# The last two parts of a convolution's x and C by seven products ahead of retention, with their weight sums made in DRAM

## The chip, the cores and the metric

One Trainium2 chip, one core. The time is device microseconds of one execution of the whole kernel; the kernel before has three timed runs. A profiled execution, timed apart from these, gives the trace. TensorE is called PE, VectorE DVE, ScalarE ACT, GpSimd POOL and SyncE SP.

## What is computed

One layer of a hybrid encoder for x of 512 tokens x 1024 channels, in float32. Cut to what matters here:

```python
h = rmsnorm(x, g_mix)
xc, gb, gc, q, k, v, g_sw, gate_a, gate_r = split(h @ w_in)       # 11 x 1024 columns
u = gc * xc
conv = sum over 3 taps of u_pad[:, tap:tap + s] * w_conv[tap]      # depthwise, along the tokens
y_a = (gb * conv) @ w_a_out
ret = retention of 4 heads (q, k rotated; scores with decay; @ v)  # both directions
y_r = (groupnorm(ret) * g_ret * silu(g_sw)) @ w_r_out
x = x + (sigmoid(gate_a) * y_a + sigmoid(gate_r) * y_r) @ w_o
x = x + swiglu(rmsnorm(x, g_ffn))                                  # 2816 wide
y = rmsnorm(x, g_final)
```

The change touches xc and gc (called x and C below), gb (called B) and the order in which they are worked out beside the retention.

## The kernel before

**Numbers.** Every matrix product is made of three matmuls: both operands are split into a rounded part hi and a remainder lo, and hi·hi, hi·lo and lo·hi are added up in PSUM (`mm3` and `prod`). A weight unit of 128 x 1024 goes from DRAM by SP's queue into a `raw` buffer (10 of them), ACT casts it to `whi` (L196) and DVE subtracts to get `wlo` (L197); five buffers of each exist. The same helper `split` makes hi and lo of activations.

**Products.** The plain ones take blocks of weights from `wpack`: `feature_major` gives 256 columns of a projection, with features on the partitions, as 2 x 24 matmuls of 128x512 (two units of weights); `token_major` gives an output product in four PSUM banks, 96 matmuls of 128x512 for 1024 columns in two halves. The others make a 2x2 block product by seven products instead of eight. `fm_quad` does it with features on the partitions: its seven calls of `prod` have 24 matmuls of 128x256 each, 168 in all, one unit of weights each, and it yields 256 columns of two projections at once, for both halves of the tokens. Their weights are `b11`, `b21`, `b22` and the sums `t1` to `t4` of quarters of w_in. For all quads but two, DVE adds the two raw quarters of a sum in SBUF (L300). For the first two pairs of the FFN (`SUMMED`) the sums are made in DRAM ahead of time by POOL's queue: `sum_step` issues one step from the list `steps` (a copy at L273, or an addition at L271), each put behind a store with `issue_after`. A step on a sum waits for the step before it on the same sum. The seven products write three PSUM banks (a, d, b); between products, ACT copies a bank into a `t512` buffer (`snap`, L432). There are nine `t512` buffers; the z stores read from them too.

**Stages.** The stages run in this order: projections q and k of three heads; six token-major quads for v, the head gates and the merge gates (`do_quad`, with the `sum_step` calls); `mix_quads`; the retention heads, with the last two parts of the convolution between them; output product of the convolution by `strassen`; merge; w_o; FFN; final norm.

The convolution is cut into four parts of 256 columns. In `mix_quads` three `fm_quad`s make x and C of part 0, x and C of part 1, and B of both parts; `conv` (L737 on ACT, L739 on DVE) applies the taps, and `z_forms` makes the sums of z = B * conv that the output product needs, splits them into t512 buffers and stores them to DRAM by POOL's queue (`store`, L601). Parts 2 and 3 are made by `do_mix(s)`: three `feature_major` calls with x, C and B, 48 matmuls of 128x512 each; x is snapped, C is multiplied with it (L774), the taps are applied, and B multiplies the result (L779).

The order of the heads is: `load_head(0)`, scores of head 0 (`do_scores`, 24 matmuls; DVE L833), `do_mix(2)`, and then for each head h: load of head h+1, `do_pv(h)` (48 matmuls; normalisation by DVE at L854 to L859), scores of head h+1, `do_t(h)` (16 transposes on DVE at L211, then splits with DVE at L200), and behind that `do_mix(3)` for h = 0, or else the output product wr(h-1) of the head before (`do_wr`, 96 matmuls).

**What sets the order.** Each engine works in the order of its own queue. The weights' order is the list `plan()`, taken one chunk at a time, split two units ahead and loaded four entries ahead. A scheduler places the instructions of all engines from the program's order and its priorities, so the order around a change is that of the built program.

Of the kernel before, what the change touches and what calls it, by code (L numbers as in the profile page):

```python
# [1 line left out]

# [1 line left out]

# [32 lines left out]
QH = CH // 2  # L37
# [33 lines left out]
def plan():  # L71
# [8 lines left out]
    def a(name, col):  # L80
        out.append(("c", name, 0, 8, col, 256))
# [16 lines left out]
            a("w_in", C_K + h * QK)  # L98
    for c in (0, 512):
        quad(C_GA + c, C_GR + c)  # L100
    for c0, c1 in ((C_XC, C_GC), (C_XC + 256, C_GC + 256), (C_GB, C_GB + 256)):
        for name in FORMS:
            out.append(("q", ("x", c0, c1), name, 0, 4))
    for s in (2, 3):
        for c in (C_XC, C_GC, C_GB):
            a("w_in", c + s * 256)
    for h in range(HEADS):
        for c in (0, 512):
            b("w_r_out", h * VD, 4, c, 512)
# [34 lines left out]

SUMMED = (("f", 0), ("f", 1))


def loads():  # L150
# [17 lines left out]
def block_kernel(ctx: ExitStack, tc: tile.TileContext, xT, xtok, wpack, wquad, cols, decs, rot, g_ffn, g_final, out):  # L168
# [45 lines left out]
    pos = [0]  # L214
    block = [0]

    made = []
    ready = []

# [8 lines left out]
    def prefetch_block(pieces, loads, splits, inbig):  # L228
        i = block[0]
        block[0] += 1  # L230
        st = [rawtile(), rawtile()]
        units = []
        per = max(1, pieces // 2)
        m = QH // per
        for c, (o, n) in enumerate(((0, 512), (512, 512), (QH, QH)) if pieces > 2 else ((0, QH), (QH, QH))):
            if loads:
                loads(c)
            nc.sync.dma_start(st[o // QH][:, o % QH:o % QH + n], wpack[i][:, o:o + n])
        for half in range(2):
# [16 lines left out]
    def quarter(quad, name, u=0):  # L256
        return wquad[next(i for i, x in enumerate(QUARTERS) if x[1:4] == (quad, name, u))]

    steps = [(quad, f, g, add) for group in (
        (("t1", "b11", 0), ("t3", "b22", 0)), (("t1", "b12", 1), ("t3", "b12", 1)),  # L260
        (("t2", "t1", 0),), (("t2", "b22", 1),), (("t4", "t2", 0),), (("t4", "b21", 1),))
        for quad in SUMMED for f, g, add in group]

    def sum_step(behind=None):

# [334 lines left out]
    def store(dst, t):  # L600
        return nc.gpsimd.dma_start(dst, t)  # L601
# [103 lines left out]
    def do_quad(left, right, func, func_left=None):  # L705
        def ev_sum(dst, o, f):
            def ev(tt, t):
                if f:
                    nc.scalar.activation(t, t, f)
                last = store(dst[:, o + tt, :], t)  # L710
                if tt and not o:
                    sum_step(last)
            return ev

        def ev21(tt, ps):
            t = t512()
# [32 lines left out]
    def z_forms(s, z):  # L749
# [3 lines left out]
        def put(j, t):  # L753
# [11 lines left out]
        put(2, w)  # L765
        put(3, x2[:, 1:2])

    def do_mix(s):
        us, c = [], bigtile()[:, 0:2, :]
        feature_major(xg, lambda m, ps: us.append(snap(ps)))  # L770
        u = u_tile()

        def ev_c(m, ps):
            nc.vector.tensor_tensor(out=u[:, m, 1:513], in0=ps, in1=us[m], op=ALU.mult)  # L774
            conv(m, 2 * s + m, u[:, m], c[:, m])
        feature_major(xg, ev_c)

        def ev_b(m, ps):
            nc.vector.tensor_tensor(out=c[:, m], in0=ps, in1=c[:, m], op=ALU.mult)  # L779
        feature_major(xg, ev_b)  # L780
        z_forms(s, c)

    T1, T2 = slice(0, 256), slice(256, 512)

    def halves(t):
        return t.rearrange("p (m t) -> p m t", m=2)

    def mix_quads():

        c = bigtile().rearrange("p (s m) t -> p s m t", s=2)  # L790
        for s in range(2):
            u, got = u_tile(), {}

            def ev21(ps):
                nc.vector.tensor_tensor(out=u[:, :, 257:513], in0=halves(ps), in1=halves(got["c2"]), op=ALU.mult)

            def ev12(t):
                nc.vector.tensor_tensor(out=u[:, :, 1:257], in0=halves(got["x1"]), in1=halves(t), op=ALU.mult)
            fm_quad(xf, lambda t: got.update(x1=t), ev21, lambda t: got.update(c2=t), ev12)
            for m in range(2):  # L800
                conv(m, 2 * s + m, u[:, m], c[:, s, m])

        def times(s, t):
            def ev(b):
# [3 lines left out]
        fm_quad(xf, times(0, T1), times(0, T2), times(1, T2), times(1, T1))  # L808
        for s in range(2):
            z_forms(s, c[:, s])  # L810


    def load(src, dt=F32):
        t = bigtile(dt)
        nc.sync.dma_start(t if dt == F32 else t.bitcast(F32), src)
        return t

    def load_head(h):
# [79 lines left out]
    mix_quads()  # L898
    nxt = load_head(0)
    p = do_scores(nxt[0], nxt[1])  # L900
    vv, sg = split_v(nxt[2]), nxt[3]
    do_mix(2)
# [403 lines left out]
```

## Time and profile before

| | us |
|---|---|
| timed runs, median of 3 | 1028.52 |
| timed runs, lowest and highest | 1028.49, 1029.9 |
| profiled execution, its own time | 1031.7 |
| its span | 1029.9 |
| mean clock of PE granted in it | 0.996 |

The span is what the trace covers; the profiled execution's own time is 1.8 us longer, for what lies around it. In the views that follow, a group's row has its busy time, the mean of one instruction in ns, and behind the second bar the idle time of its engine ahead of it and what ended most of that. A row of the timeline has start, length, engine, line and operation; in square brackets stands the idle time before it and what ended it. The chain of work that ended last is followed back from the last instruction. A row of the table by stages gives, for a stretch of time, the busy time and the number of instructions of PE, PE's weight loads, DVE, ACT and POOL, then the clock that PE was granted (1.00 is full), the share of the DMA engines' time and what they moved in GB/s. The heads stage begins at 386.6 us and the output product of the convolution at 605.2 us.

### The profile page before, as it was taken

The page shows a single profiled execution, that of the slowest core. Times are in us where ns is not written, and L with a number is a line of the kernel's source. Part 1 is how long each engine was busy: PE and PEld are TensorE (multiplying, and loading weights), DVE is VectorE, ACT ScalarE, POOL GpSimd, SP SyncE. Part 2 cuts the span into 40 slices and gives each one's busy share as a digit, 9 for nine tenths or more (in the row PEclk, how much of TensorE's full clock was granted, in tenths as well). Part 3 has the DMA queues.
Part 4 walks back from the last instruction along what each step waited for, and adds up shares of the span by engine and source line. Part 5 has one row for each costly group of instructions (what it writes and reads, how often), then busy time and mean ns, then how long its engine had stood idle before and what let it go on. Part 6 is the DMA issues. An engine that isn't in the chain of part 4 may idle for free.

```text
span 1029.9 us, 14786 instructions
## 1 busy us (share of the span) xinstructions
PE 1018.8 (99%) x5616; PEld 890.0 (86%) x5616; DVE 885.7 (86%) x1145; ACT 534.0 (52%) x723; POOL 125.2 (12%) x205
## 2 busy tenths in 40 slices
PE   8999999999999999999999999999999999999997
PEld 7888888888888998888888888889998999899985
DVE  7778898979798888797989998569998999889996
ACT  6546655653655455343543234356654565556553
POOL 0030221222122003202011000000002000110011
PEclk9999999999999999999999999999999999999999
DMA  9424587695767657818177525633318522663422
GB/s 342 181 74 176 199 275 224 207 305 175 239 192 246 245 194 272 333 60 333 47 281 276 211 91 180 232 108 113 127 45 220 178 83 82 198 152 102 164 33 91
DMA packets 51448, 187.66 MB, mean 182 GB/s; under 512 B 6896, under 2 KB 6896, under 8 KB 47408
## 3 DMA queue, kind: packets, MB, share of 16 engines
q1 hardware_dynamic: 36736, 133.45, 37.4%
q0 software_dynamic: 14496, 53.23, 17.4%
q8 instruction: 44, 0.72, 0.3%
q14 instruction: 28, 0.23, 0.1%
q10 hardware_dynamic: 144, 0.03, 0.0%
HBM read 148.14 MB, written 46.92 MB: 189 GB/s over the span
## 4 chain that ended last, share of the span: by engine, by line
PE 98%; DVE 1%; DMA 0%; issue 0%; POOLq 0%; POOL 0%; SPq 0%
PE bank L425 36%; PE bank L381 28%; PE bank L340 11%; PE bank L342 11%; PE bank L341 11%; DMA raw<-wpack 0%; PE bank L997 0%; PE bank L948 0%; DVE xform L197 0%; DVE big L1198 0%; DVE wlo L197 0%; DVE big L1173 0%; POOLq L1302 0%; POOL fin L1186 0%; PE bank L535 0%
## 5 line engine op out<-in xcount | busy, mean ns | idle before, releaser
L196 ACT CAST whi<-raw 128x1024 fp32r<-128x1024 f32 (+1 forms) x289 | 294.3, 1034 | 280.9 <-PE bank L425 63.7
L197 DVE TENSOR_TENSOR wlo<-raw,whi 128x1024 fp32r<-128x1024 f32 (+1 forms) x290 | 343.8, 1201 | 79.3 <-ACT whi L196 78.8
L381 PE MATMUL bank<-xform,whi 128*128 128x256 f32 x1424 | 257.5, 283 | 0.0
L381 PEld LDWEIGHTS bank<-xform,whi 128*128 128x128 f32 x1424 | 222.2, 192 | 0.9 <-ACT t L432 0.5
L381 PE MATMUL bank<-xform,wlo 128*128 128x256 f32 x712 | 201.1, 283 | 0.0
L425 PE MATMUL bank<-whi,big 128*128 128x512 f32 x596 | 187.5, 390 | 0.0
L300 DVE TENSOR_TENSOR raw<-raw 128x1024 f32<-128x1024 f32 (+1 forms) x128 | 151.9, 1204 | 3.8 <-DMA raw<-wquad 2.6
L381 PEld LDWEIGHTS bank<-xform,wlo 128*128 128x128 f32 x712 | 136.5, 192 | 0.0
L425 PEld LDWEIGHTS bank<-whi,big 128*128 128x128 f32 x596 | 111.9, 188 | 24.0 <-ACT t L432 0.4
L425 PE MATMUL bank<-whi,xform 128*128 128x512 f32 x384 | 121.1, 389 | 0.0
L425 PE MATMUL bank<-wlo,big 128*128 128x512 f32 x298 | 116.0, 389 | 0.0
L432 ACT COPY t<-bank 128x512 f32<-128x512 f32 x105 | 60.9, 585 | 56.0 <-PE bank L381 29.7
L340 PE MATMUL bank<-big,whi 128*128 128x512 f32 x224 | 87.4, 392 | 2.1 <-DVE whi L196 2.1
L342 PE MATMUL bank<-big,wlo 128*128 128x512 f32 x224 | 87.7, 393 | 0.0
L341 PE MATMUL bank<-big,whi 128*128 128x512 f32 x224 | 87.4, 392 | 0.0
L425 PEld LDWEIGHTS bank<-whi,xform 128*128 128x128 f32 x384 | 72.1, 188 | 14.9
L425 PE MATMUL bank<-wlo,xform 128*128 128x512 f32 x192 | 74.8, 390 | 0.4 <-DVE wlo L197 0.4
L340 PE MATMUL bank<-whi,big 128*128 128x512 f32 x176 | 69.0, 392 | 0.0
L341 PE MATMUL bank<-wlo,big 128*128 128x512 f32 x176 | 68.5, 389 | 0.0
L342 PE MATMUL bank<-whi,big 128*128 128x512 f32 x176 | 68.1, 390 | 0.0
L425 PEld LDWEIGHTS bank<-wlo,big 128*128 128x128 f32 x298 | 56.0, 188 | 11.4
L340 PEld LDWEIGHTS bank<-big,whi 128*128 128x128 f32 x224 | 42.3, 189 | 11.1 <-issue 2.3
(183 smaller groups left out, 1387.1 us busy)
## 6 DMA issues: line engine op xcount, KB each, us to landing
raw<-wquad SPq DMA_DIRECT2D x132, 512.0 KB, 4.7
raw<-wpack SPq DMA_DIRECT2D x51, 512.0 KB, 6.4
z<-t POOLq DMA_DIRECT2D x24, 256.0 KB, 5.6
zform<-z POOLq DMA_DIRECT2D x6, 1024.0 KB, 6.5
v<-t POOLq DMA_DIRECT2D x16, 256.0 KB, 5.1
sg<-t POOLq DMA_DIRECT2D x16, 256.0 KB, 4.7
qh<-t POOLq DMA_DIRECT2D x16, 256.0 KB, 2.8
ql<-t POOLq DMA_DIRECT2D x16, 256.0 KB, 3.5
```

Source lines behind the costliest of these rows:

```text
L196: first = (round or nc.scalar.copy)(hi, src)
L197: nc.vector.tensor_tensor(out=lo, in0=src, in1=hi.bitcast(F32), op=ALU.subtract)
L300: nc.vector.tensor_tensor(out=t, in0=t, in1=raws[quad, more, u][:, 0:n], op=ALU.add)
L340: nc.tensor.matmul(ps, lh, rh, start=first, stop=False)
L341: nc.tensor.matmul(ps, lh, rl, start=False, stop=False)
L342: nc.tensor.matmul(ps, ll, rh, start=False, stop=last)
L381: nc.tensor.matmul(o, l[:, c], r[:, k], start=start and s == 0 and k == 0 and i == 0, stop=stop and k == 3 and i == 2, skip_group_check=True)
L425: nc.tensor.matmul(pss[tt], l, r[:, c], start=start and k == 0 and i == 0, stop=stop and k == n - 1 and i == 2, skip_group_check=True)
L432: nc.scalar.copy(t, ps)
```

## The change

x and C of parts 2 and 3 become two more `fm_quad`s (`xc_quad(2)` and `xc_quad(3)`), run in `mix_quads` behind the three that were there and behind `z_forms` of parts 0 and 1; `load_head(0)` is called between the two, and the loads of later weight blocks are put behind its last load (`behind`). Their results stay in a second big tile (`cs[1]`). `do_mix(s)` keeps B alone, one `feature_major` of 48 matmuls, and `z_forms`. The sums of weights of both new quads are made in DRAM, ahead of those of the FFN, so that `steps` has 32 entries in place of 16. `sum_step` is called once more in each `do_quad` (four times rather than three) and after each of the four stores in `z_forms`; the FFN's sums are thereby made partly between the z stores. Each new quad loads seven units of weights (two quarters more are read in DRAM for the sums) where part 2 or 3 had four for x and C.

```diff
-    for c0, c1 in ((C_XC, C_GC), (C_XC + 256, C_GC + 256), (C_GB, C_GB + 256)):
+    for c0, c1 in ((C_XC, C_GC), (C_XC + 256, C_GC + 256), (C_GB, C_GB + 256),
+                   (C_XC + 512, C_GC + 512), (C_XC + 768, C_GC + 768)):
         for name in FORMS:
             out.append(("q", ("x", c0, c1), name, 0, 4))
     for s in (2, 3):
-        for c in (C_XC, C_GC, C_GB):
-            a("w_in", c + s * 256)
+        a("w_in", C_GB + s * 256)
...
-SUMMED = (("f", 0), ("f", 1))
+XC = tuple(("x", C_XC + o, C_GC + o) for o in (512, 768))
+
+SUMMED = (*XC, ("f", 0), ("f", 1))
...
-            nc.sync.dma_start(st[o // QH][:, o % QH:o % QH + n], wpack[i][:, o:o + n])
+            with tc.issue_after(behind[-1].ins) if behind else nullcontext():
+                nc.sync.dma_start(st[o // QH][:, o % QH:o % QH + n], wpack[i][:, o:o + n])
...
-    steps = [(quad, f, g, add) for group in (
-        (("t1", "b11", 0), ("t3", "b22", 0)), (("t1", "b12", 1), ("t3", "b12", 1)),
-        (("t2", "t1", 0),), (("t2", "b22", 1),), (("t4", "t2", 0),), (("t4", "b21", 1),))
-        for quad in SUMMED for f, g, add in group]
+    def sums_of(quads):
+        return [(quad, f, g, add) for group in (
+            (("t1", "b11", 0), ("t3", "b22", 0)), (("t1", "b12", 1), ("t3", "b12", 1)),
+            (("t2", "t1", 0),), (("t2", "b22", 1),), (("t4", "t2", 0),), (("t4", "b21", 1),))
+            for quad in quads for f, g, add in group]
+
+    steps = sums_of(SUMMED[:2]) + sums_of(SUMMED[2:])
...
-                if tt and not o:
+                if tt:
                     sum_step(last)
...
             for d, x in zip(zd[j], hl):
-                store(d[:, :, s, :], x.bitcast(F32))
+                last = store(d[:, :, s, :], x.bitcast(F32))
+            sum_step(last)
...
-    def do_mix(s):
-        us, c = [], bigtile()[:, 0:2, :]
-        feature_major(xg, lambda m, ps: us.append(snap(ps)))
-        u = u_tile()
-
-        def ev_c(m, ps):
-            nc.vector.tensor_tensor(out=u[:, m, 1:513], in0=ps, in1=us[m], op=ALU.mult)
-            conv(m, 2 * s + m, u[:, m], c[:, m])
-        feature_major(xg, ev_c)
-
-        def ev_b(m, ps):
-            nc.vector.tensor_tensor(out=c[:, m], in0=ps, in1=c[:, m], op=ALU.mult)
-        feature_major(xg, ev_b)
-        z_forms(s, c)
+    def xc_quad(s, c):
+
+        u, got = u_tile(), {}
+
+        def ev21(ps):
+            nc.vector.tensor_tensor(out=u[:, :, 257:513], in0=halves(ps), in1=halves(got["c2"]), op=ALU.mult)
+
+        def ev12(t):
+            nc.vector.tensor_tensor(out=u[:, :, 1:257], in0=halves(got["x1"]), in1=halves(t), op=ALU.mult)
+        fm_quad(xf, lambda t: got.update(x1=t), ev21, lambda t: got.update(c2=t), ev12)
+        for m in range(2):
+            conv(m, 2 * s + m, u[:, m], c[:, m])
...
         for s in range(2):
             z_forms(s, c[:, s])
-
+        xc_quad(2, cs[1][:, 0])
+        head = load_head(0)
+
+        behind.append(last[-1])
+        xc_quad(3, cs[1][:, 1])
+        return head
+
+    def do_mix(s):
+
+        c = cs[1][:, s - 2]
+
+        def ev_b(m, ps):
+            nc.vector.tensor_tensor(out=c[:, m], in0=ps, in1=c[:, m], op=ALU.mult)
+        feature_major(xg, ev_b)
+        z_forms(s, c)
```

Lines behind the diff's middle are eight to twenty higher in the changed kernel: L196 and L197 become L198 and L199, L340 to L342 become L348 to L350, L381 becomes L389, L601 becomes L609, L271 and L273 become L279 and L281, L211 becomes L213, L200 becomes L202, L779 becomes L826, L833 becomes L853.

Three places of the engines' orders matter for what follows. A row has line, operation, what it writes and what it reads, and the shape; names end in a buffer's number.

The first is DVE behind the scores of head 2, at the transposes of head 1 (`big_4384`). In the kernel before:

```order
L197 TENSOR_TENSOR big_4379<-big_4244,big_4378 128x1024
L197 TENSOR_TENSOR big_4333<-t512_4374,big_4332 128x512
L211 STREAM_TRANSPOSE big_4384<-big_3839 32x4x4x32 x16
L197 TENSOR_TENSOR wlo_4494<-raw_4486,whi_4493 128x1024
L200 SCALAR_TENSOR_TENSOR big_4402<-big_4384,cols_sb_89,big_4401 128x512 x4
L197 TENSOR_TENSOR wlo_4731<-raw_4726,whi_4730 128x1024
```

The same place in the changed kernel, where the transposes write `big_4595`:

```order
L199 TENSOR_TENSOR big_4544<-t512_4585,big_4543 128x512
L199 TENSOR_TENSOR big_4590<-big_4455,big_4589 128x1024
L213 STREAM_TRANSPOSE big_4595<-big_4190 32x4x4x32 x16
L199 TENSOR_TENSOR wlo_4637<-raw_4629,whi_4636 128x1024
L199 TENSOR_TENSOR wlo_4701<-raw_4696,whi_4700 128x1024
L202 SCALAR_TENSOR_TENSOR big_4613<-big_4595,cols_sb_97,big_4612 128x512 x4
L199 TENSOR_TENSOR wlo_4705<-raw_4697,whi_4704 128x1024
```

In both, one subtraction of a weight unit stands right behind the transposes. In the kernel before the units of wr0 were `wlo_4149`, `wlo_4153`, `wlo_4422` and `wlo_4426`, all of them ahead of this place, so that `wlo_4494` belongs to the next product. In the changed kernel wr0's units are `wlo_4360`, `wlo_4364`, `wlo_4633` and `wlo_4637`; the last of them has moved behind the transposes.

The second is PE in wr0, in the changed kernel, where the third unit of weights (`whi_4632`, `wlo_4633`) gives way to the fourth (`whi_4636`, `wlo_4637`):

```order
L348 MATMUL bank_4695<-whi_4632,big_4345 128x512
L349 MATMUL bank_4695<-wlo_4633,big_4345 128x512
L350 MATMUL bank_4695<-whi_4632,big_4346 128x512
L348 MATMUL bank_4692<-whi_4636,big_4345 128x512
L348 MATMUL bank_4693<-whi_4636,big_4345 128x512
L348 MATMUL bank_4694<-whi_4636,big_4345 128x512
L348 MATMUL bank_4695<-whi_4636,big_4345 128x512
L349 MATMUL bank_4692<-wlo_4637,big_4345 128x512
L350 MATMUL bank_4692<-whi_4636,big_4346 128x512
```

The four matmuls that need only `whi_4636` have moved ahead of the first one that needs `wlo_4637`; behind `wlo_4705` DVE's order is again that of the kernel before.

The third is POOL's queue at the z stores of parts 0 and 1, with nothing but stores in the kernel before:

```order
L601 DMA z020_222<-t512_3477 256x1x256
L601 DMA z120_223<-t512_3478 256x1x256
L601 DMA z021_224<-t512_3487 256x1x256
L601 DMA z022_226<-t512_3493 256x1x256
L601 DMA z121_225<-t512_3488 256x1x256
L601 DMA z013_228<-t512_3499 128x256
L601 DMA z122_227<-t512_3494 256x1x256
L601 DMA z113_229<-t512_3500 128x256
L601 DMA z020_222<-t512_3507 256x1x256
```

In the changed kernel the steps of the FFN's sums stand between them (`t2f0` is the sum t2 of FFN pair 0; L281 copies, L279 adds):

```order
L609 DMA z020_230<-t512_3502 256x1x256
L609 DMA z120_231<-t512_3503 256x1x256
L281 DMA t2f0_90<-t1f0_89 16x8192
L609 DMA z021_232<-t512_3513 256x1x256
L609 DMA z121_233<-t512_3514 256x1x256
L281 DMA t2f1_94<-t1f1_93 16x8192
L609 DMA z022_234<-t512_3520 256x1x256
L609 DMA z122_235<-t512_3521 256x1x256
L279 DMA t2f0_90<-wquad 64x2048
L609 DMA z013_236<-t512_3527 128x256
L609 DMA z113_237<-t512_3528 128x256
L279 DMA t2f1_94<-wquad 64x2048
```

After every two stores one step has moved in; the copy of `t2f0` stands ahead of the addition to it, and that ahead of the copy into `t4f0`.

More of the change, by code (lines that the diff above doesn't have):

```diff
@@ L1 @@
-from contextlib import ExitStack
+from contextlib import ExitStack, nullcontext
 import numpy as np
@@ L215, in block_kernel @@
     block = [0]
+    behind = []
     made = []
@@ L786, in halves @@
         return t.rearrange("p (m t) -> p m t", m=2)
+    def xc_quad(s, c):
[7 more added lines that the diff above has]
+            conv(m, 2 * s + m, u[:, m], c[:, m])
+    cs = []
     def mix_quads():
-        c = bigtile().rearrange("p (s m) t -> p s m t", s=2)
+        for _ in range(2):
+            cs.append(bigtile().rearrange("p (s m) t -> p s m t", s=2))
+        c = cs[0]
         for s in range(2):
[L792 to L801, printed above, removed]
+            xc_quad(s, c[:, s])
         def times(s, t):
@@ L810, in mix_quads @@
             z_forms(s, c[:, s])
+        xc_quad(2, cs[1][:, 0])
[9 more added lines that the diff above has]
+        z_forms(s, c)
+    last = []
     def load(src, dt=F32):
         t = bigtile(dt)
-        nc.sync.dma_start(t if dt == F32 else t.bitcast(F32), src)
+        last.append(nc.sync.dma_start(t if dt == F32 else t.bitcast(F32), src))
         return t
@@ L896, in do_wr @@
             token_major(yr, 0, 1, ev)
-    mix_quads()
-    nxt = load_head(0)
+    nxt = mix_quads()
     p = do_scores(nxt[0], nxt[1])
```

## The prediction

> **What bounds the kernel now.** I read the page's shares, then the chain of work that ended last, then the waits of TensorE.
>
> ```profile
> PE 1018.8 (99%) x5616; PEld 890.0 (86%) x5616; DVE 885.7 (86%) x1145; ACT 534.0 (52%) x723; POOL 125.2 (12%) x205
> PE 98%; DVE 1%; DMA 0%; issue 0%; POOLq 0%; POOL 0%; SPq 0%
> PE bank L340 <- DVE whi L196: 2.1, 1, 2.1
> PE bank L473 <- DVE lw L658: 1.0, 1, 1.0
> PE bank L425 <- DVE wlo L197: 0.4, 1, 0.4
> 326.49 55.14 PE bank L381 x456
> 605.23 38.08 PE bank L425 x168
> ```
>
> PE makes 98% of the chain and waits 3.5 us in all. So today each matmul less is time less, as long as PE is fed. The two chain rows are stretches of matmuls without a gap. They give the price of one: 38.08 / 168 = 226.7 ns for 512 columns, 55.14 / 456 = 120.9 ns for 256. The second thing to see is DVE at 86%: there is not much room behind PE. How much there is depends on the stage, and the table by stages shows it (span, PE, PEld, DVE, ACT, POOL busy, clock, DMA share, GB/s):
>
> ```profile
> 80.00:320.00 240.00, 239.60 (x1058) 198.07 (x1057) 208.68 (x225) 139.71 (x177) 50.10 (x88) 1.00 0.70 223
> 326.50:386.60 60.10, 60.10 (x491) 59.20 (x491) 54.15 (x65) 30.59 (x40) 4.09 (x7) 1.00 0.63 217
> 438.30:509.40 71.10, 71.10 (x315) 58.90 (x314) 62.98 (x97) 28.37 (x39) 7.57 (x13) 1.00 0.41 150
> ```
>
> These are the token-major quads with the sums in DRAM, the three quads of the convolution, and the stretch from the second head's scores to the end of the first output product's weights, with part 3 of the convolution in it.
>
> **Step 1, PE's own work.** Per part, 96 matmuls of 512 columns become 168 of 256: 96 x 0.2267 = 21.8 us against 168 x 0.1209 = 20.3 us. Two parts save 2 x 1.45 = 2.9 us. This is the whole gain.
>
> The Trainium skill ("TensorE: Matmul & The Clock Gate", section "Back-to-back issue gap") states a sustained spacing of about 131 ns at 512 columns and 81 ns at 128. An estimate by a straight line between its figures is 98 ns at 256, and by these the change would cost 2 x (168 x 98 - 96 x 131) ns = 7.8 us of PE rather than save any. The trace disagrees (226.7 and 120.9 ns), so the rows decide.
>
> **Step 2, the heads.** The gain of step 1 is not the main effect. PE loses 2 x 21.8 = 43.5 us of work between the heads, while most of what DVE did beside it stays. The groups of DVE in the stretch 438.3 to 509.4 (busy, mean ns, idle before and what ended it):
>
> ```profile
> L211 DVE STREAM_TRANSPOSE big<-big 32x512 f32<-32x512 f32 x32 | 22.5, 702 | 0.4
> L197 DVE TENSOR_TENSOR wlo<-raw,whi 128x1024 fp32r<-128x1024 f32 x7 | 8.6, 1222 | 3.2 <-ACT whi L196 3.1
> L833 DVE SCALAR_TENSOR_TENSOR t<-bank,tab 128x512 f32<-128x512 f32 x8 | 5.4, 685 | 0.4 <-PE bank L342 0.4
> L739 DVE SCALAR_TENSOR_TENSOR big<-u,cols_sb,big 128x512 f32<-128x512 f32 x4 | 3.0, 746 | 0.0
> L779 DVE TENSOR_TENSOR big<-bank,big 128x512 f32<-128x512 f32 x2 | 1.4, 692 | 1.1 <-PE bank L342 1.1
> L774 DVE TENSOR_TENSOR u<-bank,t 128x512 f32<-128x512 f32 x2 | 1.4, 684 | 0.0
> L197 DVE TENSOR_TENSOR t<-big,t 128x256 fp32r<-128x256 f32 x1 | 0.4, 427 | 2.4 <-DMA z<-t 2.4
> ```
>
> The two heads' transposes (22.5 us), the scores, the normalisation and the forms of z all stay. What leaves is two L774 (1.4), four L739 (3.0) and five of the seven subtractions of weight units, which the changed order has ahead of this stretch or behind it, 5 x 1.22 = 6.1 us: 10.5 in all. DVE is busy 62.98 us in 71.10, idle 8.1; of that idle time the waits named above make 0.4 + 3.2 + 0.4 + 1.1 + 2.4 = 7.5. So the work left is 71.1 - 7.5 - 10.5 = 53.1 us.
>
> PE's side: in the changed order, from the first scores matmul of head 1 to the first that reads the last weight unit of wr0, there stand 24 (scores) + 48 (B) + 48 (pv) + 24 (scores) + 72 + 4 (wr0) = 220 matmuls, 220 x 0.2267 = 49.9 us. That last unit's subtraction stands on DVE right behind the second transposes, as the rows of the order in the section on the change show; in the kernel before it was the unit of another chunk that stood there:
>
> ```profile
> 438.31 0.68 DVE L833 SCALAR_TENSOR_TENSOR t<-bank,tab 128x512 f32<-128x512 f32 x1
> 436.59 0.23 PE bank L340
> 496.77 11.44 DVE L211 STREAM_TRANSPOSE big<-big 32x512 f32<-32x512 f32 x16
> 508.25 1.23 DVE L197 TENSOR_TENSOR wlo<-raw,whi 128x1024 fp32r<-128x1024 f32 x1
> ```
>
> DVE takes up the scores 438.31 - 436.59 = 1.7 us after PE starts them. So the unit is ready 1.7 + 53.1 = 54.8 us after PE's start, where PE wants it at 49.9: PE waits **4.9 us**, if DVE itself never waits. The floor of this term is 4.9. Above it come the 2.4 us that DVE waits for a z store's buffer, which now falls in a shorter stage, and up to 1.8 us if DVE enters the stage late after conv, splits and B of part 2. The ends are 4.9 and 9.1; I take **7**, the middle. A part of it shows as a wait for wr0's PSUM banks, which the normalisation of pv1 frees. Behind these rows both orders agree, so the delay is carried to the end.
>
> **Step 3, the quads and the stores of z.** The fourth quad begins where the third ends, and its first snaps need t512 buffers that the z stores hold. Today's scores hide this (two waits of ACT, POOL's second store, and times from issue to landing):
>
> ```profile
> 395.37 0.62 ACT L196 CAST t<-t 128x512 fp32r<-128x512 f32 x1 [3.29 <-DMA z<-t]
> 398.82 0.62 ACT L196 CAST t<-t 128x512 fp32r<-128x512 f32 x1 [2.83 <-DMA z<-t]
> 385.09 0.68 POOL L601 DMA_DIRECT2D z<-t  x1 [0.43 <-DVE t L197]
> z<-t POOLq DMA_DIRECT2D x24, 256.0 KB, 5.6
> t2f<-t1f POOLq DMA_DIRECT2D x2, 512.0 KB, 6.1
> t2f<-wquad POOLq DMA_DIRECT2D x2, 512.0 KB, 8.9
> t4f<-t2f POOLq DMA_DIRECT2D x2, 512.0 KB, 5.2
> ```
>
> ACT already waits 3.29 and 2.83 us for z stores. Now eight steps of the FFN sums stand between these stores on POOL. Each copy or addition waits for the one before it in its chain: 6.1, then 8.9, then 5.2 us. From the second store's end, 385.1 + 0.7 = 386, the third step of a chain is issued at 386 + 6.1 + 8.9 = 401, and whatever stands behind it waits with it. PE reaches the fourth quad's third product, which overwrites the bank that its first snap reads, at 326.5 + 3 x 20.3 + 11.2 (93 x 0.1209: three products of its own and 21 matmuls of the fifth quad, which the order puts ahead) = 398.6. The snap stands on ACT behind casts at 398.82 or later, and the next snap needs the buffer of a store that follows such a cast and lands 5.6 us later, at 404. So PE waits somewhere between nothing (if the stores drain as today and the weights' buffers are free) and 8 us (if a store behind the 401 step is the one needed: 401 + 5.6 - 398.6). I take **4**, between the two; no row decides it more closely.
>
> **Costed at nothing.** Casts and subtractions of weight units rise from 8 to 14. Per quad DVE has now (54.15 - 12 x 1.204 for L300) / 3 = 13.2 us of 20.3, since the new quads have no L300 adds:
>
> ```profile
> L300 DVE TENSOR_TENSOR raw<-raw 128x1024 f32<-128x1024 f32 (+1 forms) x128 | 151.9, 1204 | 3.8 <-DMA raw<-wquad 2.6
> ```
>
> Eight more DRAM steps fall into 80 to 320. Each reads and writes 0.5 MB, 8.4 MB in all, 38 us at the 223 GB/s of that row, against 240 x 0.30 = 72 us of idle DMA. If that cover were gone, a late sum would stall the fourth quad at its second unit. The eight steps' issue time on POOL hides in its 190 idle us there. Head 0's loads now go out between the fourth and the fifth quad, about a quad's 20.3 us ahead of the scores, against landings of 7.4 to 11.1 us:
>
> ```profile
> big<-qh SPq DMA_DIRECT2D x4, 1024.0 KB, 7.4
> big<-sg SPq DMA_DIRECT2D x4, 1024.0 KB, 11.1
> ```
>
> **The sum.** -2.9 + 7 + 4 = +8.1 us on the profiled execution: 1031.7 + 8.1 = 1039.8. That execution was 3.2 us above the median of the runs (1028.52), so by the median I forecast **1036.6**; its ends are -2.9 + 4.9 + 0 and -2.9 + 9.1 + 8, so 1030.5 to 1042.7.
>
> **The rivals.**
> - Only the heads stall (step 3's cover holds; today PE runs through the first z stores without a wait): -2.9 + 7, **1032.6**. Against it stand ACT's two waits.
> - PE's clock falls at the new waits. The waits quoted at the start include one of 2.1 us, and behind it the clock reads:
>
> ```profile
> 7.00:11.40 4.40, 4.40 (x13) 3.44 (x14) 4.21 (x8) 4.03 (x7) 0.00 (x0) 0.62 1.03 383
> 84.29 0.50 PE L425 MATMUL bank<-wlo,xform 128*128 128x512 f32 x1 [0.40 <-DVE wlo L197]
> 84.30:88.00 3.70, 3.70 (x16) 3.09 (x17) 3.70 (x4) 2.49 (x4) 0.00 (x0) 1.00 0.00 0
> ```
>
>   A clock of 0.62 over 4.4 us loses 1.7 us; the 0.40 us wait lost none. Two or three waits of over 2 us would add 3.4 to 5.1: **1040.0 to 1041.7**. Against it: the slow clock at 7 us may come from the start of the program. The Trainium skill (the same page, "What's actually happening") says that an idle window of about 3.4 us halves the clock, and as much busy time restores it; by that only a wait in one piece of that length counts, and no row here shows one.
> - A balance: DVE gets 2 us of the stretch's work done during pv0, and step 3 costs nothing: stall 2.9, no change, **1028.5**.
> - The other side: PE stays covered in both places and the 2.9 us are gained, **1025.6**. This needs DVE's work in the stretch to be at most 49.9 - 1.7 = 48.2 us rather than 53.1, that is, over four more subtractions ahead of the second transposes. DVE was idle 8.1 us in the stretch, so it is not full today; but the idle time is already taken off above.
>
> That the change does not do what it says is excluded: the order shows both quads ahead of the scores.
>
> **Chances.** Forecast 0.52, heads only 0.17, clock 0.12, balance 0.08, faster 0.11. A measurement of this kernel can tell about 0.2% (2 us) from no change. Faster 0.11, same 0.08, slower 0.81. The range reaches from the balance to the upper end of step 3's bound with a little of the clock, 1028.0 to 1043.5; it leaves out the faster rival and a few hundredths above.
>
> **What would show it.** Step 1: 168 matmuls per new quad at 0.121 us without gaps. Step 2: waits of PE at wr0's first or last weight unit, behind DVE's transposes, of 5 to 9 us; wrong if PE runs through from the second scores to wr0's end. Step 3: a wait of PE in the fourth quad for ACT's snap, with ACT waiting for z stores; wrong if PE runs through or if the wait is for weights from DRAM. The clock: PEclk below 1.00 behind these waits. Were the sums in DRAM late, PE would wait in the fourth or fifth quad for a load of t1 to t4, and the whole reckoning would be too low.

## The result, and the profile after

| | median us | lowest and highest | runs |
|---|---|---|---|
| before | 1029.9 | 1028.49, 1030.16 | 5 |
| changed | 1055.52 | 1053.29, 1056.79 | 5 |

The ratio is 1.0248, with a 95% interval of 1.0234 to 1.0262: the changed kernel is 25 us slower. The prediction had the sign and said 1036.6 in a range up to 1043.5. The profiled execution took 1056.34 us, 24.6 more than that of before.

The page's shares and chain of the changed kernel, as they were shown of before:

```profile
PE 1024.6 (97%) x5760; PEld 900.5 (85%) x5760; DVE 894.3 (85%) x1157; ACT 541.2 (51%) x731; POOL 134.3 (13%) x221
PE 81%; DVE 10%; DMA 4%; issue 3%; ACT 1%; POOL 1%; POOLq 0%; SPq 0%; DVEq 0%; ACTq 0%
```

PE's share of the chain fell from 98% to 81%. PE is busy for longer although it has less to do, which already hints at a slower clock. Its waits (in all, times, longest):

```profile
PE bank L389 <- ACT t L440: 10.4, 2, 10.1
PE bank L349 <- DVE wlo L199: 4.7, 1, 4.7
PE bank L389 <- DVE wlo L199: 2.3, 2, 1.7
PE bank L389 <- ACT whi L198: 1.3, 2, 1.1
PE bank L348 <- DVE bnmv L875: 1.2, 1, 1.2
PE bank L348 <- DVE whi L198: 1.1, 1, 1.1
PE bank L481 <- DVE lw L666: 1.0, 1, 1.0
PE bank L348 <- DVE big L879: 0.8, 2, 0.4
```

L389 is the product of the quads: 10.4 + 2.3 + 1.3 = 14.0 us are lost there, 13.2 of them in the fourth and fifth quad and 0.8 in the ones ahead. The 4.7, 1.2 and 0.8 are lost at wr0, 6.7 us. The two that are left, 2.1 us, are the program's start; the kernel before waited 3.5 us in all, so 1.4 more. The table by stages shows where the clock goes down:

```profile
387.00:430.00 43.00, 29.80 (x205) 28.56 (x205) 20.31 (x29) 13.79 (x20) 14.30 (x21) 0.80 1.02 365
480.00:560.00 80.00, 73.38 (x311) 59.26 (x310) 74.23 (x121) 34.77 (x52) 10.28 (x18) 0.96 0.60 227
```

At the prices of the prediction (0.1209 and 0.2267 us) the 205 matmuls of 256 columns of the first would take 24.8 us and take 29.8; the 311 of 512 columns of the second would take 70.5 and take 73.4. So 5.0 + 2.9 = 7.9 us go to the clock. The account closes: -2.9 (fewer matmuls) + 14.0 + 6.7 + 7.9 - 1.4 = 24.3 us, against 24.6 measured. The first row also has DMA at its full share and 365 GB/s.

The long wait in the fourth quad, from the timeline of the changed kernel:

```profile
400.39 0.62 ACT L198 CAST t<-t 128x512 fp32r<-128x512 f32 x1 [3.28 <-DMA z<-t]
...
405.16 0.69 DVE L199 TENSOR_TENSOR t<-t,t 128x512 fp32r<-128x512 f32 x1 [5.48 <-DMA z<-t]
...
407.13 0.62 ACT L198 CAST t<-t 128x512 fp32r<-128x512 f32 x1 [6.12 <-DMA z<-t]
...
412.02 0.69 DVE L199 TENSOR_TENSOR t<-t,t 128x512 fp32r<-128x512 f32 x1 [6.17 <-DMA z<-t]
...
412.75 0.58 ACT L440 COPY t<-bank 128x512 f32<-128x512 f32 x1 [4.69 <-DVE t L199]
...
413.38 0.80 PE L389 MATMUL bank<-xform,whi 128*128 128x256 f32 x2 [10.12 <-ACT t L440]
413.98 0.41 PE L389 MATMUL bank<-xform,wlo 128*128 128x256 f32 x1
```

and the step of its chain ahead of these, with POOL's first wait for a step of the sums:

```profile
394.81 17.08 DMA z<-t
...
402.90 0.83 POOL L279 DMA_DIRECT2D t2f<-wquad  x1 [6.42 <-DMA t2f<-t1f]
```

Read it from the end: PE waits for ACT's snap (L440), the snap for a t512 buffer that DVE reads at 412.02, and that subtraction for a buffer whose z store was issued at 394.81 and landed 17.08 us later. Ahead of that ACT and DVE had waited for z stores before, ACT 3.28 and 6.12 us and DVE 5.48. The store that ended the wait was on its way before POOL waited for any step of the sums: in this stretch that first happened ahead of the step at 402.90, for 6.42 us. So it was issued without such a wait, and what was late is its landing. Behind the wait PE's matmuls are slow: the two of the row at 413.38 take 0.6 us rather than 0.24.

The heads, on DVE and PE:

```profile
518.25 11.45 DVE L213 STREAM_TRANSPOSE big<-big 32x512 f32<-32x512 f32 x16
529.73 2.36 DVE L199 TENSOR_TENSOR wlo<-raw,whi 128x1024 fp32r<-128x1024 f32 x2
...
531.00 0.79 PE L349 MATMUL bank<-wlo,big 128*128 128x512 f32 x1 [4.66 <-DVE wlo L199]
...
532.02 0.63 PE L349 MATMUL bank<-wlo,big 128*128 128x512 f32 x1
```

This is the place that the prediction named: wr0's last weight unit, behind the second transposes. The matmuls behind the wait are 0.43 us apart, not 0.227.

### The profile page after: what moved, and what is told of

It reads as the page before. It is cut to its first block, busy times and chain, and to the rows that moved or that the text cites. A ratio compares the mean times of both kernels' runs of the same rounds, so it can differ in the third digit from the quotient of the medians.

```text
span 1054.6 us, 15127 instructions
## 1 busy us (share of the span) xinstructions
PE 1024.6 (97%) x5760; PEld 900.5 (85%) x5760; DVE 894.3 (85%) x1157; ACT 541.2 (51%) x731; POOL 134.3 (13%) x221
## 4 chain that ended last, share of the span: by engine, by line
PE 81%; DVE 10%; DMA 4%; issue 3%; ACT 1%; POOL 1%; POOLq 0%; SPq 0%; DVEq 0%; ACTq 0%
PE bank L433 33%; PE bank L389 25%; PE bank L349 7%; PE bank L350 7%; PE bank L348 7%; DMA z<-t 2%; DVE big L213 2%; DVE wlo L199 2%; DVE big L199 1%; DMA ga<-t 1%; DVE big L747 1%; ACT whi L198 1%; DVE raw L308 1%; DVE t L853 1%; POOL z L609 0%
## 5 line engine op out<-in xcount | busy, mean ns | idle before, releaser
L198 ACT CAST whi<-raw 128x1024 fp32r<-128x1024 f32 (+1 forms) x295 | 300.5, 1034 | 290.6 <-PE bank L433 62.4
L199 DVE TENSOR_TENSOR wlo<-raw,whi 128x1024 fp32r<-128x1024 f32 (+1 forms) x296 | 350.7, 1202 | 81.2 <-ACT whi L198 80.7
L389 PE MATMUL bank<-xform,whi 128*128 128x256 f32 x1552 | 283.4, 285 | 10.7 <-ACT t L440 10.4
L389 PEld LDWEIGHTS bank<-xform,whi 128*128 128x128 f32 x1552 | 244.0, 194 | 12.4 <-ACT t L440 11.5
L389 PE MATMUL bank<-xform,wlo 128*128 128x256 f32 x776 | 220.5, 285 | 0.0
L389 PEld LDWEIGHTS bank<-xform,wlo 128*128 128x128 f32 x776 | 150.1, 194 | 0.0
L440 ACT COPY t<-bank 128x512 f32<-128x512 f32 x107 | 61.9, 585 | 58.0 <-PE bank L389 31.0
L433 PE MATMUL bank<-wlo,xform 128*128 128x512 f32 x192 | 74.8, 390 | 0.0
L348 PE MATMUL bank<-whi,big 128*128 128x512 f32 x176 | 69.1, 395 | 2.0 <-DVE bnmv L875 1.2
L350 PE MATMUL bank<-whi,big 128*128 128x512 f32 x176 | 69.2, 396 | 0.0
L433 PEld LDWEIGHTS bank<-wlo,big 128*128 128x128 f32 x298 | 56.0, 188 | 11.4
L348 PE MATMUL bank<-big,whi 128*128 128x512 f32 x160 | 63.0, 396 | 1.1 <-DVE whi L198 1.1
L350 PE MATMUL bank<-big,wlo 128*128 128x512 f32 x160 | 62.7, 394 | 0.0
L349 PE MATMUL bank<-big,whi 128*128 128x512 f32 x160 | 62.6, 394 | 0.0
L198 ACT CAST big<-t 128x512 fp32r<-128x512 f32 (+1 forms) x60 | 34.4, 579 | 26.1 <-DVE t L1072 12.1
```

The lines of the kernel that those rows point to most:

```text
L198: first = (round or nc.scalar.copy)(hi, src)
L199: nc.vector.tensor_tensor(out=lo, in0=src, in1=hi.bitcast(F32), op=ALU.subtract)
L348: nc.tensor.matmul(ps, lh, rh, start=first, stop=False)
L349: nc.tensor.matmul(ps, lh, rl, start=False, stop=False)
L350: nc.tensor.matmul(ps, ll, rh, start=False, stop=last)
L389: nc.tensor.matmul(o, l[:, c], r[:, k], start=start and s == 0 and k == 0 and i == 0, stop=stop and k == 3 and i == 2, skip_group_check=True)
```

## The experiments

All ratios are to runs of the kernel before on the same chip. Theories for the quads' term were Q (POOL's queue: the steps of the sums hold the z stores) and D (too much DMA in these 40 us); F (the order of the z forms and the snap) came when Q fell. For the heads they were H (DVE has more work than PE) and its rivals.

**1. e1_sums_later: the sums out of the z stores of parts 0 and 1.**

```diff
-            sum_step(last)
+            if s >= 2:
+                sum_step(last)
```

> The changed kernel with the eight FFN sum steps that stood between the z stores of parts 0 and 1 put between those of parts 2 and 3. In the changed kernel PE waits 13 us in the fourth quad and loses about 5 us more to a lower clock behind it. Theory Q (POOL's queue: each step waits for the step before it on the same sum, and the z stores behind it wait along): the wait falls to 0 to 3 us, the clock stays at 1.00 there, and the time goes from 1055.5 to about 1038 (1035 to 1041). Theory D (too much DMA at once, the loads of head 0 above all; the sums are a part of it only): the wait falls to 5 to 8 us, time 1044 to 1051.

Measured: 1057.26 us, ratio 1.0259 [1.024, 1.0278]. Nothing was won. Its longest waits of PE:

```profile
PE bank L389 <- ACT t L440: 6.1, 1, 6.1
PE bank L349 <- DVE wlo L199: 5.6, 1, 5.6
PE bank L389 <- DVE wlo L199: 4.7, 2, 4.2
```

and the stage of the quads in the table:

```profile
387.00:430.00 43.00, 31.03 (x220) 29.83 (x219) 21.48 (x31) 16.40 (x23) 9.04 (x14) 0.84 0.74 280
```

With no sum between the stores the quads still lose 12.4 us (6.1, 4.7 and 1.6 for casts). Theory Q falls as the cause by itself; the 5 to 8 us and the time that theory D gave did not come either. The steps seem to cost in their new place: PE waits 8.5 us at wr0 rather than 6.7, and 1.8 us for loads of a later head, for which the changed kernel doesn't wait.

**2. e2_head_early: head 0's loads ahead of the z forms.**

```diff
+        head = load_head(0)
         for s in range(2):
             z_forms(s, c[:, s])
         xc_quad(2, cs[1][:, 0])
-        head = load_head(0)
```

> The changed kernel with load_head(0) ahead of z_forms of parts 0 and 1, so that 4 MB are loaded before these stores. Theory Q: POOL's queue is as before, the wait in the fourth quad stays at 10 to 14 us, time 1053 to 1057. Theory D: the DMA share there falls from 1.02 to about 0.75, the z stores land in 7 us or less, the wait falls by 6 to 10 us, time 1043 to 1049.

Measured: 1047.84 us, ratio 1.0168 [1.0147, 1.019], 8 us better. In the quads PE waits 9.3 us:

```profile
PE bank L389 <- ACT t L440: 6.0, 2, 5.7
PE bank L389 <- ACT whi L198: 1.7, 2, 1.1
PE bank L389 <- DVE wlo L199: 1.6, 2, 1.0
```

The loads are a part of it, as theory D has it, and the time is in its range. But the share of DMA did not fall to 0.75 (0.97 in 387 to 430), the wait fell by 4.7 us and not by 6 to 10, and more than half of it is left. At wr0 4.6 us are left; the waits of 1.2 and 0.8 us for its banks went too, which is a part of the 8 us.

**3. e4_one_part: as 1, and only part 2 by a quad.** The plan, `SUMMED` and `mix_quads` have part 2 alone, and for part 3:

```diff
+        if s == 3:
+            us = []
+            feature_major(xg, lambda m, ps: us.append(snap(ps)))
...
+            feature_major(xg, ev_c)
```

> As e1_sums_later, but only part 2's x and C by a quad; part 3's stay between the heads as 2 x 48 matmuls of 128x512. Theory H (in the heads DVE has more work than PE): the 6.7 us of waits at wr0 and the 2.9 us of lower clock behind them vanish, against 1.45 us more PE work: 7 to 9 us under e1_sums_later, about 1030. Rival (the waits at wr0 come from elsewhere, the weights' loads or the sums between the stores of parts 2 and 3): the waits stay, 1 to 2 us above e1_sums_later.

Measured: 1041.21 us, ratio 1.0109 [1.0093, 1.0126], 16 us under 1. In the heads only 0.8 us of waits are left, the largest of them 0.6; in the quads it still waits:

```profile
PE bank L390 <- ACT t L441: 9.6, 3, 7.4
...
PE bank L349 <- ACT big L921: 0.6, 1, 0.6
```

The heads' term hangs on part 3's matmuls between them, as forecast. The gain is larger than the 7 to 9 us expected, since one quad less also shortens the quads' waits.

**4. e5_unit_first: as 1, wr0's last weight unit ahead of the transposes.**

```diff
+        if h == 1:
+            prefetch()
         new = do_t(h, t)
```

> As e1_sums_later, with one call of prefetch() ahead of the second transposes, so that the subtraction of wr0's last weight unit stands ahead of them on DVE. Theory H (DVE is short of time in all of the stage): the wait at wr0 goes but comes back at the next scores or output product, time within 2.5 us of e1_sums_later. Rival O (only the place of this one subtraction counts): 4.7 us of wait and about 2.9 us of clock are saved, 6 to 8 us under e1_sums_later.

Measured: 1056.33 us, ratio 1.0254 [1.023, 1.0277], the same as 1. The wait has only moved:

```profile
PE bank L348 <- ACT big L912: 5.0, 1, 5.0
```

L912 is ACT's copy of wr0's banks. It stands on ACT behind the splits of the transposed head, and these wait for DVE's transposes. The matmul that waits, at 537.44 us, reads no weights: wr0's 96 matmuls run through behind their first wait, and it is `do_pv(2)` behind wr0 that waits for wr0's banks to be copied out. So the wait came back in the product that follows, at the next thing behind the transposes. The time is as theory H said, the place one product earlier.

**5. e6_z_between: z forms of part 1 behind the fourth quad.**

```diff
-        for s in range(2):
-            z_forms(s, c[:, s])
+        z_forms(0, c[:, 0])
         xc_quad(2, cs[1][:, 0])
+        z_forms(1, c[:, 1])
```

> The changed kernel with z_forms of part 0 ahead of the fourth quad and z_forms of part 1 behind it (before: both ahead of it); sums and loads untouched. Theory F (the fourth quad's first snap stands on ACT behind the casts of both z_forms, and these need two turns of the nine t512 buffers, each as long as a z store takes to land): the waits in the fourth and fifth quad fall from 13 us to 4 or less, the clock stays near 1.00, time 1038 to 1044. Theory D (too much DMA in these 40 us): the same stores, sums and loads run, the waits stay at 9 us or more, time over 1048.

Measured: 1046.56 us, ratio 1.0167 [1.0149, 1.0184]. The fourth quad now runs through; of the two new quads only the fifth still waits, once, for the same kind of snap:

```profile
411.50 0.62 ACT L198 CAST t<-t 128x512 fp32r<-128x512 f32 x1 [7.52 <-DMA z<-t]
...
419.71 0.80 PE L389 MATMUL bank<-xform,whi 128*128 128x256 f32 x2 [6.22 <-ACT t L440]
```

Theory F is right that the order decides who waits, theory D that a z store still takes long: ACT waits 7.52 us for one. Neither range held; each has about half.

**6 to 8. The three together, and in pairs.** e7_quads_clear has the order of 5, the loads of 2 and the sums behind the loads of the merge gates:

```diff
-            sum_step(last)
...
-        nc.gpsimd.dma_start(t, d)
+        sga_load = nc.gpsimd.dma_start(t, d)
+    while steps:
+        sum_step(sga_load)
     do_wr(HEADS - 1, yr)
```

> As e6_z_between, with load_head(0) ahead of z_forms of part 0 and the eight FFN sum steps behind the loads of the merge gates, after the last head. If order, loads and sums are all of the quads' term: no wait over 1 us in the quads, clock 1.00 there, the waits of 5 to 7 us at wr0 and the clock behind them stay: 1034 to 1039. If something else holds the fourth quad: waits of 4 us or more there, 1042 or over.

e11_order_and_loads leaves the sums between the z stores:

> As e7_quads_clear, but with the FFN sum steps between the z stores, as in the changed kernel (so: z forms of part 0 and 1 apart, head 0 loaded early). With the order right and no surge of DMA, the sums should cost little if they only fill POOL's queue: wait in the quads 0 to 2 us, 1034 to 1038. If the sums hold the z stores by themselves: 3 to 7 us of waits there, 1038 to 1044.

e12_order_and_sums leaves the loads late:

> As e7_quads_clear, but with load_head(0) behind z forms of part 1, as late as in e6_z_between (so: order right, sums out of the way, 4 MB of head 0 loaded between the quads). If the loads alone hold the z stores and the scores: 3 to 7 us of waits in the quads or at the first scores, 1038 to 1044. If they cost little once sums and order are right: 1034 to 1038.

| kernel | z forms apart | head 0 early | sums later | ratio | PE's waits in the quads, us | clock, 387 to 430 | landing of a z store, us |
|---|---|---|---|---|---|---|---|
| changed | | | | 1.0248 | 14.0 | 0.80 | 7.4 |
| e1 | | | yes | 1.0259 | 12.4 | 0.84 | 9.0 |
| e2 | | yes | | 1.0168 | 9.3 | 0.88 | 5.4 |
| e6 | yes | | | 1.0167 | 6.7 | 0.88 | 7.4 |
| e12 | yes | | yes | 1.0088 | 1.9 | 1.00 | 6.5 |
| e11 | yes | yes | | 1.0049 | 2.1 | 1.00 | 5.1 |
| e7 | yes | yes | yes | 1.0045 | 1.4 | 1.00 | 3.5 |

The medians are 1034.38 us for e7 (interval of the ratio 1.0031 to 1.0059), 1034.91 for e11 (1.0031 to 1.0067) and 1038.32 for e12 (1.0073 to 1.0103). The landing is the median of the kernel's 24 stores of 256 KB. In e7 all of the 1.4 us are in the three old quads, and the two new ones run through; in e11 and e12 1.0 and 0.9 us are left in the new ones. e7's time came as expected, with 4.1 us at wr0 rather than 5 to 7, and e11 by its first case. e12 lies on the border of its two cases; its waits in the quads are short, and a part of its 4 us over e7 is at wr0, 6.3 us of waits against 4.1.

The table tells three things. Without the order no row is under 9 us of waits; but loads early and sums later were not run together in the old order, so it is not shown that the order is needed. With it, either the early loads or the later sums are enough for the quads. And the sums alone, which the prediction took for the cause, are worth nothing without the order (e1), 8 us with it and late loads (e6 to e12), and nothing again once the loads are early (e11 to e7).

The early loads shorten the landing of a z store in every pair of rows, and so do the later sums in the new order. The landing alone does not decide: with 5.4 us (e2) the quads wait, with 6.5 (e12) they hardly do. Nor does the share of DMA decide how long a store takes: in 387 to 430 us it is 0.74 in e1, with 9.0 us, and 1.01 in e11, with 5.1. So theory D's "too much DMA" is right about the loads, but what it is in them that lengthens a landing is not shown. The rows behind the first and the last figure, first of the changed kernel, with two steps of the sums:

```profile
z<-t POOLq DMA_DIRECT2D x24, 256.0 KB, 7.4
t2f<-t1f POOLq DMA_DIRECT2D x2, 512.0 KB, 8.3
t2f<-wquad POOLq DMA_DIRECT2D x2, 512.0 KB, 14.7
```

and of e7_quads_clear:

```profile
z<-t POOLq DMA_DIRECT2D x24, 256.0 KB, 3.5
```

**9. e8_pool_subtracts: as 6, eight subtractions of weight units on POOL.**

```diff
-            nc.vector.tensor_tensor(out=lo, in0=src, in1=hi.bitcast(F32), op=ALU.subtract)
+            (sub or nc.vector).tensor_tensor(out=lo, in0=src, in1=hi.bitcast(F32), op=ALU.subtract)
...
+made.append(split(..., sub=nc.gpsimd if wr and half else None))
```

> As e7_quads_clear, with the subtraction of every second weight unit of the four output products wr (8 units) on POOL rather than DVE. Theory H (DVE has more work than PE between the heads): 8 x 1.2 us less for DVE, the waits at wr0 fall from about 7 us to 2 or less and the clock stays up, time 1027 to 1031. Rival P (POOL is too slow at this, over 6 us a unit, or slows DVE): new waits for these units, not under e7_quads_clear.

Measured: 1035.71 us, ratio 1.0059 [1.0042, 1.0076], not under e7. Its subtractions on POOL, from the groups, and then its longest wait of PE:

```profile
L199 POOL TENSOR_TENSOR wlo<-raw,whi 128x1024 fp32r<-128x1024 f32 x8 | 19.9, 2491 | 77.8 <-ACT whi L198 77.8
```

```profile
PE bank L348 <- ACT big L910: 3.9, 1, 3.9
```

POOL takes 2.49 us for what DVE does in 1.2, and PE does not wait for it. But from the timeline, right ahead of the transposes:

```profile
496.36 2.65 POOL L199 TENSOR_TENSOR wlo<-raw,whi 128x1024 fp32r<-128x1024 f32 x1 [5.02 <-ACT whi L198]
496.64 3.46 DVE L199 TENSOR_TENSOR big<-big 128x1024 fp32r<-128x1024 f32 x1
```

A subtraction of DVE took 3.46 us rather than 1.2 while POOL made one of its own, so the transposes started at 500.0, against 498.4 in e7. DVE was not relieved ahead of them, and the wait moved to ACT's copies behind them, as in 4. Two other subtractions of DVE that ran beside one of POOL took 2.27 and 1.75 us. Rival P has the second half of its condition (POOL slows DVE). Theory H's 2 us or less did not come, although DVE was busy for less time in all from 480 to 560 us, 70.1 us against 74.8 in e7: the units taken off it there had stood behind the transposes.

**10. e10_turn_later: as 6, the transposes of head 1 behind wr0.**

```diff
-        new = do_t(h, t)
+        if h != 1:
+            new = do_t(h, t)
...
             do_wr(h - 1, yr)
+        if h == 1:
+            new = do_t(h, t)
```

> As e7_quads_clear, with the transposes of head 1 (do_t(1)) behind wr0 rather than ahead of it; nothing is left out or made cheaper. Theory O2 (the wait is the place of 11.4 us of transposes ahead of things that wr0 needs: in e7 its last weight unit, in e5 and e8 ACT's splits of the transposed head ahead of the copies that free wr0's banks): the 4 us at wr0 and the slow clock behind go, and no other wait over 1 us comes, 1027 to 1031. Theory H (DVE as a whole is short between the heads): the wait comes back at wr1 or the third scores, 1033 to 1037.

Measured: 1031.69 us, ratio 1.0021 [1.0011, 1.0031], 2.5 us under e7 by the ratios. Half of the wait went, half came back behind the transposes' new place:

```profile
506.71 1.23 DVE L199 TENSOR_TENSOR wlo<-raw,whi 128x1024 fp32r<-128x1024 f32 x1 [3.73 <-ACT whi L198]
507.86 11.45 DVE L213 STREAM_TRANSPOSE big<-big 32x512 f32<-32x512 f32 x16
519.33 1.30 DVE L873 BATCH_NORM_STATS2 bnst<-bank 128x6 f32<-128x512 f32 x2
...
525.00 0.47 PE L348 MATMUL bank<-whi,big 128*128 128x512 f32 x1 [2.18 <-DVE bnmv L875]
...
525.78 0.63 PE L348 MATMUL bank<-whi,big 128*128 128x512 f32 x1
```

DVE had even waited 3.7 us ahead of them, for a weight unit of the next product that stood in front. Neither theory had this time; it left H and O2 open.

**11. e13_turn_in_wr: as 6, the transposes between the two halves of wr0.**

```diff
             token_major(yr, 0, 1, ev)
+            if between and half == 0:
+                between()
...
-            do_wr(h - 1, yr)
+            do_wr(h - 1, yr, turn if h == 1 else None)
```

> As e7_quads_clear, with the transposes of head 1 between the two halves of wr0: behind its last weight unit on DVE, ahead of the next product's units, and ACT's splits of them behind the copies of the first half. Nothing is left out or made cheaper. Theory O2 (the place of the transposes decides): no wait over 1 us between 430 and 631, clock 1.00 there, so both parts' 2.9 us less the 1 to 2 us left in the quads: 1027 to 1029.5. Theory H (DVE short as a whole): a wait of 2 us or more moves to the third scores, wr1 or the second half of wr0: 1031 to 1036.

Measured: 1029.34 us, ratio 0.9995 [0.9986, 1.0004]. PE's only wait in the heads, and then the heads in the table:

```profile
PE bank L349 <- DMA big<-ql: 1.0, 1, 1.0
```

```profile
480.00:560.00 80.00, 79.00 (x349) 65.09 (x348) 78.34 (x131) 33.95 (x50) 13.61 (x25) 1.00 0.57 206
```

The other waits are 2.2 us at the program's start, 0.4 in the products ahead of the quads and 0.9 in the three old quads. The two new quads run through, from the chain:

```profile
381.01 40.94 PE bank L389 x334
```

DVE is 98% busy from 480 to 560 us, and PE waits for it nowhere in the heads. It is the same work in another order: theory H falls as a statement on the whole stage, O2 holds. The time is in O2's range, but by the ratio it can't be told from no change.

**12 and 13. One part by a quad, with the quads clear.** The kernel of 6 with part 3 as in 3, run twice (e9 and e14):

> As e7_quads_clear, but only part 2's x and C by a quad (part 3's between the heads, as before). Theory H: no wait at wr0; with the quads clear the one quad's 1.45 us are a gain, 1027 to 1031. Rival: waits over 2 us anywhere between 326 and 605, 1033 or more.

> The kernel of e9_one_part_clear once more, beside e13_turn_in_wr on the same chip, to have its gain of 1.5 us (one quad's worth) at closer bounds: 1027.5 to 1029.5, and above e13_turn_in_wr by up to 1.4 us if that one is free of waits.

Measured: 1028.54 us, ratio 0.9986 [0.9977, 0.9995], and 1028.11 us, ratio 0.9985 [0.9977, 0.9994]. Apart from the program's start PE waits once in the second run, for 0.4 us, and not at all in the first. By the ratios the kernel is 1.4 and 1.5 us under the one before, with 0.5 to 2.4 us inside the intervals; one quad saves 1.45 in matmuls. The second run was expected above e13 and came 1.2 us under it, within what the intervals leave open. Of all versions it is the only one whose interval lies under 1.

## Why the prediction was wrong

**Step 1 was right.** The sum gave the two new quads 2 x 20.3 = 40.6 us, and where they run through (11) they take 40.9. With one quad and no waits (12 and 13) the kernel gains about that quad's 1.45 us.

**Step 2 was right in place and size.** It said 7 us (4.9 to 9.1) at wr0's last weight unit and its banks; 6.7 us were measured there. Its sum holds as well. From DVE's first row of the scores of head 1 to the end of wr0's last unit it reckoned 53.1 us of work; in the changed kernel the stretch begins with the second of these rows:

```profile
472.54 0.43 DVE L199 TENSOR_TENSOR t<-big,t 128x256 fp32r<-128x256 f32 x1 [2.73 <-DMA z<-t]
...
477.51 0.68 DVE L853 SCALAR_TENSOR_TENSOR t<-bank,tab 128x512 f32<-128x512 f32 x1
```

It ends at 529.73 + 1.2 = 530.9, so it is 53.4 us long, with 0.3 us of idle time. Of what it put above the floor of 4.9, DVE's wait for a z store came, 2.73 us just ahead of that row. That 7 was so close is in part luck, since no row had sized the middle of the range. What the sum hid is that the order decides and not the amount: 4 put one unit ahead of the transposes and the wait came back at the next thing behind them, and 11 put them behind wr0's units, with DVE 98% busy, and it was gone.

**Step 3 is the step that failed.** It said 4 us, "somewhere between nothing ... and 8 us", and 14.0 were measured, 13.2 of them in the two new quads. The kind of wait was right: ACT's snap behind work that waits for z stores. The landing time of a store was mis-sized. The upper end took a store held on POOL's queue until 401 and 5.6 us for its landing, 406.6 in all. The store that ended the wait was issued at 394.81, with no sum waiting ahead of it, and took 17.1 us. The 5.6, 6.1 and 8.9 us came from the profile of before; in the changed kernel, where the sums, the stores and 4 MB of head 0 run together, the same medians are 7.4, 8.3 and 14.7. It also counted one turn of the buffers, where ACT and DVE each have two long waits for a store.

**"Costed at nothing" failed with it.** Head 0's loads were looked at for whether they arrive in time, and they do. What they slow was not asked. Moving them alone gives 8 us back (2), with the quads' waits 4.7 us shorter.

**The clock was a rival at 0.12 with 3.4 to 5.1 us; it came with 7.9.** The row of before that it rested on (0.62 behind a wait of 2.1 us) speaks for every case with such waits, so the term belonged in the sum, not beside it.

The chance of slower, 0.81, was borne out. The sum said +8.1 us on the profiled execution and +24.6 came, 16.5 more: 10.0 from step 3, 7.9 from the clock, -0.3 from step 2 and -1.4 from waits of before that this execution had less of, which leaves 0.3. The upper end of the range was too low because its landing times were those of the profile of before and because it had only 0.8 us for the clock.

Not shown: whether more than nine t512 buffers would have done as well as the order, which no run tried.

## What to carry to other kernels

When a change moves transfers together, don't carry landing times over from the profile of before: the slowest z store of the kernel before landed in 8.2 us, and one of the changed kernel took 17.1. Ask of each moved load what it slows, not only whether it is in time. A long block on an in-order engine (here 11.4 us of transposes) is a matter of place: see what stands behind it on its own queue and on the queues that wait for it, before making anything cheaper. And take work out of a stage only as far as its covered engines allow: one part of two is shown to gain, about what its matmuls save; for both, even with the waits gone (11), no gain is shown.

## What the runs showed of the hardware

The clock halves behind waits of about 2 us already, though not behind all of them, and for how long does not follow the length of the wait. In the changed kernel the 10.12 us wait is followed by about 6 us at half the clock, the 4.66 us wait by 4.4 us of matmuls at 0.43 us each. In e4 a wait of 7.40 us is followed by 3.0 us at 0.50, in e8 one of 3.88 by 5.5 us. In all versions each wait of 3.88 us or more was followed by the half clock. In e10 a wait of 2.18 us was enough, and the matmuls slow down 0.8 us after it; in e1 a wait of 2.08 us at wr0 left the clock at 1.00. Half of a slow stretch is lost, so about 1.5 to 3 us behind each. In the changed kernel two shorter waits in a row did it as well, from its timeline:

```profile
397.16 0.51 PE L389 MATMUL bank<-big,whi 128*128 128x256 f32 x2 [1.06 <-ACT whi L198]
399.40 0.58 PE L389 MATMUL bank<-big,wlo 128*128 128x256 f32 x1 [1.73 <-DVE wlo L199]
399.78 0.63 PE L389 MATMUL bank<-big,whi 128*128 128x256 f32 x2
```

The stretch behind the 10.12 us wait, in the table of the changed kernel:

```profile
413.30:418.80 5.50, 5.42 (x25) 5.42 (x26) 0.69 (x1) 0.14 (x2) 1.94 (x3) 0.50 0.98 386
```

The Trainium skill ("TensorE: Matmul & The Clock Gate", section "What's actually happening") has the clock halved after an idle window of about 3.4 us and restored after as much busy time. The 4.66 and 10.12 us waits agree. The 2.18 us wait, and 1.06 and 1.73 us within 3.3 us, do not fit a rule that asks for 3.4 us of idle time in one piece; the slow stretches of 3 to 6 us are near the length that it gives or longer.
